# Zeroing the gate buffers beside the scans and the output projection, and more expert tiles beside each head's search, in a hybrid encoder block with product-key experts

## The chip, the core and the metric

One core of a Trainium2 chip runs the whole kernel. Its engines are TensorE (PE, matmul; PEld its weight loads), VectorE (DVE), ScalarE (ACT), GpSimd (POOL) and SyncE (SP). SP, ACT and GpSimd also issue DMAs, which 16 DMA engines carry out. The metric is the device time of one execution in microseconds.

## What is computed

One layer over 1024 tokens of width 1024, in float32. Four heads of a gated delta rule and four of an mLSTM are scanned forward and backward in chunks; then come an output projection and a layer of single-neuron experts that are found by product keys:

```
h = rmsnorm(x); p = h @ w_in                     # gq gk gv gz, mq mk mv mo and small gates
y = concat(gdn(conv(gq,gk,gv), gz), mlstm(mq,mk,mv,mo))   # chunked, both directions summed
x = x + y @ w_out
h2 = rmsnorm(x)
for each of 8 heads:                             # peer
    s = (h2 @ w_q) @ sub_keys                    # 2 x 128 scores a token
    16 best of each half -> 16 best of their sums: idx in 128*128, gate = softmax(best)
x = x + sum over heads and picks: gate * gelu(h2 . u_tab[idx]) * v_tab[idx]
out = rmsnorm(x)
```

## The kernel before

The 1024 tokens are eight blocks of 128. The kernel text is a plain sequence, but the builder reorders it: a planner with a model of each engine and queue sets the order in which each engine's instructions stand, and every engine then runs its own list in that order, waiting on semaphores. Two means in the text bind the planner: `tc.issue_after(x)` puts what is issued inside it behind instruction x on its engine's list, and `tc.keep_in_program_order` keeps a GpSimd DMA in the order of the text.

Front. `split_w` (L109) loads 128 columns of w_in, splits them into a high and a low part (`whi` on ACT at L116, `wlo` on GpSimd at L120), and 48 matmuls into two tiles `psP` make a projection (L127, three products for every pair). `conv_tile` (L401) evicts them to `xp`, and DVE runs the five-tap conv as five operations (L408, L412). For the delta rule's k and q, `to_rows` transposes (`psR`, L420), DVE normalises, and `psB` (L441) transposes back. `amat` (L449) then makes, for each chunk n, products `pkk` and `pqk`, and for each direction a unit: loads `dec` and `bb` from the row buffer rowb (three buffers each), GpSimd adds a mask (L460), ACT takes four exponentials (L463), GpSimd multiplies (L464), DVE multiplies with `pkk` and `pqk` (L465, L470), and ACT issues six stores (L466 to L471). `invert` (L481) inverts 32-wide diagonal blocks on DVE in 31 dependent steps, for the first four chunks and then for the last four, and stores them in `yinv`. Projections for mk, mq, the two output gates, mv and gv follow. Then `levels` (tiles `psX`, `psI`) completes the inverses, one step ahead of the scans `delta` (L625) and `mlstm` (L693), 8 steps in 2 directions. `project` (L823) makes the output projection and the second norm, block by block.

Expert stage. The blocks have two kinds. For two of them (AL) each token's 2 x 128 expert rows are gathered by GpSimd (`gather`, L1011) and summed on DVE. The other six (BL) use all 16384 experts densely: for each of 128 tiles i of 128 experts, `act_steps` (L1072) multiplies the split tile of u_t (`uh` on ACT, `ul` on DVE) with the blocks' transposed h2 in 48 matmuls `pa`, ACT takes the gelu, and the result is stored in gesc; `early_tile` is one such tile. Their gates form matrices of expert by token. For four of the six (NS = 4) these lie in DRAM as `gd`, which has to be zero at first; GpSimd scatters 8 x 16 x 4 = 512 columns into them (`scatter`, L1110). For the last two, `psg` matmuls build them.

`router_topk` does the search of a set of blocks, head by head: `scores` (matmuls `psq` with a split w_q, `pss` with the keys), then `between(h)`, then `select`, a long chain on DVE with two products `gm` on GpSimd (L956). `between` is where expert tiles and scatters are put beside a head: KTILE = 3 tiles a head for BL, each with KSCAT / KTILE = 7 scatters of the heads before; ATILE = 1 tile a head for AL, with ASCAT = 7 scatters. That makes 24 and 8 tiles. The 96 tiles left come after, each with USCAT = 3.3 scatters and UGATH = 1.8 gathers, the first 64 of them woven among the `psg` matmuls. The output phase then loads gesc and the gates tile by tile (`gt` from `gd`) and multiplies with v, the matmuls `held` and `po`.

The zeroing: `fills` lists 32 pieces of gd of 1 MB, and `fill(n)` (L102) issues n of them on ACT's queue from a zero tile. Each of the 32 weight splits called with the name w issues one, behind its `whi` copy.

Of the kernel before, what the change touches and what calls it, by code (L numbers as in the profile page):

```python
# [8 lines left out]
F32 = mybir.dt.float32  # L9
# [5 lines left out]
AF = mybir.ActivationFunctionType  # L15
# [3 lines left out]
P = 128  # L19
# [13 lines left out]
GPAD = 16  # L33
HELD = 3
VROWS = 4
ATILE, KTILE = 1, 3
KSCAT, ASCAT, USCAT = 21, 7, 3.3
UGATH = 1.8
OTOK = 4
PACE = 8  # L40
PSG, ATB, BTB = 4, 11, 6
# [21 lines left out]
def kernel(ctx, tc, x, norm1_g, w_in, conv_w, gdn_a_log, gdn_dt_bias, gdn_norm_g,  # L63
# [3 lines left out]
    V, A, G, T = nc.vector, nc.scalar, nc.gpsimd, nc.tensor  # L67
    dma = nc.sync.dma_start
    dmas = nc.scalar.dma_start
# [21 lines left out]
    cst = pool(ctx, "cst")  # L91
    ident = cst.tile([P, P], F32, name="ident")
    epsc = cst.tile([P, 1], F32, name="epsc")
    V.memset(epsc, EPS)
    tcol = cst.tile([P, 1], F32, name="tcol")
    G.iota(tcol, pattern=[[0, 1]], base=0, channel_multiplier=1, allow_small_or_imprecise_dtypes=True)
# [2 lines left out]
    gd = [scratch(f"gd{b}", [P * PITCH, 1]) for b in range(NS)]  # L99
    fills = [(b, i) for b in range(NS) for i in range(0, NK, 16)]  # L100

    def fill(n):  # L102

        for b, i in fills[:n]:
            dmas(gd[b].rearrange("(j c) o -> j (c o)", j=P)[:, i * P:(i + 16) * P].rearrange("j (a c) -> j a c", c=512),
                 zero[:, None, :].to_broadcast([P, 4, 512]))
        del fills[:n]

    def split_w(pl, src, c0, n, name="w", bufs=2, rbufs=2, raw=None):  # L109

        if raw is None:
            raw = pl.tile([P, KD, n], F32, name=f"{name}raw", bufs=rbufs)
        dma(raw, src[:, c0:c0 + n].rearrange("(k p) c -> p k c", p=P))
        hi = pl.tile([P, KD, n], F32R, name=f"{name}hi", bufs=bufs)
        lo = pl.tile([P, KD, n], F32R, name=f"{name}lo", bufs=bufs)
        cp = A.copy(hi, raw).ins  # L116
        if name == "w":
            with tc.issue_after(cp):
                fill(1)
        G.tensor_tensor(lo, raw, hi.bitcast(F32), op=OP.subtract)  # L120
        return hi, lo

# [32 lines left out]
    with ExitStack() as st:  # L155
# [6 lines left out]
        for l in (0, 5, 6, 7):  # L162
            a = tp.tile([P, P], I32, name=f"a{l}")
            b = tp.tile([P, P], I32, name=f"b{l}")
# [43 lines left out]
    with ExitStack() as st:  # L208
# [8 lines left out]
        for t in range(NT):  # L217
            xt = fr.tile([P, D], F32, name="xt", bufs=4)
# [4 lines left out]
            ssq = fr.tile([P, 1], F32, name="ssq", bufs=4)  # L223
# [26 lines left out]
        dma(gat, gsb)  # L250

    wp = pool(st_p, "wp", side="right")
    zero = wp.tile([P, 512], F32, name="zero")
    G.memset(zero, 0.0)
    st_w = ExitStack()
    wx = pool(st_w, "wx", side="right")
    gq = ExitStack()
# [367 lines left out]
    def delta(step, d):  # L625
        Y = Ys[step, d]
        n = chunk_of(d, step)
# [20 lines left out]
        for h in range(NH):  # L648
            T.matmul(pv[:, h], Y[:, h], R[:, h], start=True, stop=True)
        vn = gw.tile([P, NH, P], F32, name="vn")  # L650
        A.copy(vn, pv)
        yield
        if step < NT - 1:
            kd = gw.tile([P, NH, P], F32, name="kd")
# [131 lines left out]
    with ExitStack() as st:  # L786
# [36 lines left out]
        def project(t, yh, yl):  # L823
            xt = wo.tile([P, D], F32, name="xt", bufs=2)
            dma(xt, x2d[t * P:(t + 1) * P])
            for c in range(2):
                ps = pp.tile([P, 512], F32, name="psO", tag="pp")
                cl = slice(c * 512, c * 512 + 512)
                mm3(ps, lambda k: yh[:, k], lambda k: yl[:, k],
                    lambda k: woh[:, k, cl], lambda k: wol[:, k, cl], KD)  # L830
                V.tensor_tensor(xt[:, cl], ps, xt[:, cl], op=OP.add)
            dmas(x2sc[t * P:(t + 1) * P], xt)
            ssq = wo.tile([P, 1], F32, name="ssq", bufs=2)
            h2 = wo.tile([P, D], F32, name="h2", bufs=2)
            A.activation(h2, xt, AF.Square, accum_out=ssq)
            A.activation(ssq, ssq, AF.Sqrt, bias=epsc, scale=1.0 / D)
            V.reciprocal(ssq, ssq)
            V.scalar_tensor_tensor(h2, xt, ssq, g2b, op0=OP.mult, op1=OP.mult)
            dmas(h2sc[t * P:(t + 1) * P], h2)
            return h2  # L840
# [501 lines left out]
```

## Time and profile before

| | |
|---|---|
| median of 3 runs | 3634.5 us (3631.62 to 3637.68) |
| the profiled execution | 3634.53 us, span of its records 3632.8 us |
| mean granted TensorE clock | 0.941 |
| busy: PE, PEld, DVE, ACT, POOL | 89%, 79%, 63%, 26%, 54% of the span |
| DMA | 745.85 MB, 205 GB/s |

Times inside the profile count from the span's start. A row of the windows gives, for one stretch, how long each engine was busy, the clock that was granted to TensorE as a share of its full speed, and the mean share that 16 DMA engines were busy. A row of a group gives the count, the busy time and the mean of one, and behind the bar how long the engine stood idle just ahead of such instructions and what ended that; "issue" means that nothing the profile shows was waited for. Matmuls overlap, so the mean of one is longer than its step in a row of many; the step is the length of such a row over its count.

### The profile page before, as it was taken

To read this page: it belongs to the slowest core of one execution; us is meant where nothing else is said; L and a number is where in the kernel's file an instruction comes from. 1 tells how busy PE (TensorE), PEld (TensorE's weight loads), DVE (VectorE), ACT (ScalarE), POOL (GpSimd) and SP (SyncE) were. 2 spreads that over 40 slices of the span, in tenths; PEclk is the share of its full clock that TensorE was granted. 3 is DMA by queue.
4 is the path that set the end of the run, shared out by engine and by line. 5 is a ranking of instruction groups with operands and counts; after the bars stand their busy time and mean duration, and the time that the engine had idled before them with its cause. 6 is when DMAs were issued, how large, how long until landed. Compare 5 with 4: busy or idle time off the path is not lost.

```text
span 3632.8 us, 46554 instructions
## 1 busy us (share of the span) xinstructions
PE 3216.3 (89%) x16847; PEld 2887.7 (79%) x16847; DVE 2304.2 (63%) x4978; ACT 933.9 (26%) x1406; POOL 1974.0 (54%) x1379
## 2 busy tenths in 40 slices
PE   7752799998996788859999998998999999999998
PEld 5541678987896788759999998998788888888887
DVE  5343803467475797965555454334788888889886
ACT  4431123424232222322222222111212212222121
POOL 1202221444168885988787787887334444444552
PEclk9865899999998899879999999999999999999999
DMA  4425365665433443447877767777999999999994
GB/s 133 134 79 129 120 197 165 174 174 167 163 69 65 73 78 90 98 103 205 235 202 221 227 178 226 207 212 231 354 329 329 330 340 334 333 322 342 342 329 174
DMA packets 489303, 745.85 MB, mean 205 GB/s; under 512 B 126480, under 2 KB 315344, under 8 KB 488560
## 3 DMA queue, kind: packets, MB, share of 16 engines
q1 hardware_dynamic: 271984, 335.68, 29.1%
q0 software_dynamic: 147456, 268.76, 26.4%
q10 hardware_dynamic: 69632, 138.43, 10.3%
q8 instruction: 132, 2.16, 0.3%
q14 instruction: 99, 0.81, 0.1%
HBM read 603.82 MB, written 138.90 MB: 204 GB/s over the span
## 4 chain that ended last, share of the span: by engine, by line
PE 56%; POOL 13%; DMA 12%; DVE 11%; issue 6%; ACT 2%; ACTq 0%; SPq 0%; DVEq 0%; POOLq 0%
PE po L1270 15%; PE held L1270 15%; PE pa L1078 10%; POOL gd L1112 10%; PE psP L127 7%; DMA g<-in_peer_u_dram,idxA 5%; PE psO L127 2%; PE psq L127 2%; POOL g L1013 2%; DVE pq L497 1%; DMA dec<-rowb 1%; POOL gm L956 1%; DMA g<-in_peer_v_dram,idxA 1%; DMA gd<-gateB,idxB 1%; DVE ul L1069 1%
## 5 line engine op out<-in xcount | busy, mean ns | idle before, releaser
L1112 POOL DMA_INDIRECT gd<-gateB,idxB x512 | 887.4, 1733 | 183.4 <-issue 143.9
L1078 PE MATMUL pa<-h2Th,ul 128*128 128x384 f32 x2048 | 537.3, 343 | 85.8 <-DVE ul L1069 85.8
L1013 POOL DMA_INDIRECT g<-in_peer_v_dram,idxA x256 | 372.9, 1457 | 413.9 <-DVE ac L1038 363.6
L1078 PE MATMUL pa<-h2Th,uh 128*128 128x384 f32 x2048 | 558.1, 354 | 0.5 <-ACT uh L1068 0.5
L1078 PE MATMUL pa<-h2Tl,uh 128*128 128x384 f32 x2048 | 533.2, 341 | 0.0
L1022 DVE CUSTOM_DVE_ANT_0 g<-g,h2A 128x1024 f32<-128x1024 f32 x256 | 311.8, 1223 | 312.2 <-DMA g<-in_peer_u_dram,idxA 312.1
L1078 PEld LDWEIGHTS pa<-h2Th,ul 128*128 128x128 f32 x2048 | 377.1, 192 | 94.1 <-DVE ul L1069 94.1
L1013 POOL DMA_INDIRECT g<-in_peer_u_dram,idxA x256 | 312.1, 1219 | 218.7 <-DVE act L1022 161.5
L1078 PEld LDWEIGHTS pa<-h2Tl,uh 128*128 128x128 f32 x2048 | 379.1, 192 | 0.0
L1038 DVE SCALAR_TENSOR_TENSOR ac<-g,act,ac 128x1024 f32<-128x1024 f32 x254 | 325.6, 1282 | 76.5 <-DMA g<-in_peer_v_dram,idxA 74.9
L1078 PEld LDWEIGHTS pa<-h2Th,uh 128*128 128x128 f32 x2048 | 363.0, 193 | 1.2 <-ACT uh L1068 1.2
L1240 ACT CAST wh<-g 128x768 fp32r<-128x768 f32 x128 | 106.4, 832 | 779.0 <-PE po L1270 629.8
L120 POOL TENSOR_TENSOR wlo<-wraw,whi 128x1024 fp32r<-128x1024 f32 x32 | 80.0, 2501 | 334.0 <-ACT whi L116 306.2
L1068 ACT CAST uh<-g 128x1024 fp32r<-128x1024 f32 x128 | 134.3, 1049 | 434.8 <-PE pa L1078 399.5
L127 PE MATMUL psP<-hTh,whi 128*128 128x512 f32 x512 | 207.2, 405 | 39.6 <-ACT mkT L521 32.4
L1270 PE MATMUL po<-h2Tl,wh 128*128 128x512 f32 x576 | 227.3, 395 | 0.0
L1270 PE MATMUL po<-h2Th,wl 128*128 128x512 f32 x576 | 227.3, 395 | 0.0
L1270 PE MATMUL po<-h2Th,wh 128*128 128x512 f32 x576 | 227.2, 394 | 0.0
L1270 PE MATMUL held<-h2Tl,wh 128*128 128x512 f32 x576 | 226.3, 394 | 0.0
L1270 PE MATMUL held<-h2Th,wl 128*128 128x512 f32 x576 | 225.8, 395 | 0.0
L1270 PE MATMUL held<-h2Th,wh 128*128 128x512 f32 x576 | 222.8, 394 | 0.0
L127 PE MATMUL psP<-hTh,wlo 128*128 128x512 f32 x512 | 205.1, 401 | 9.5 <-POOL wlo L120 9.5
(387 smaller groups left out, 6558.8 us busy)
## 6 DMA issues: line engine op xcount, KB each, us to landing
g<-in_u_t_dram SPq DMA_DIRECT2D x128, 512.0 KB, 4.2
g<-in_peer_v_dram SPq DMA_DIRECT2D x128, 512.0 KB, 6.9
gesc<-ge ACTq DMA_DIRECT2D x128, 384.0 KB, 5.3
g<-gesc SPq DMA_DIRECT2D x128, 384.0 KB, 6.2
gd<-zero ACTq DMA_DIRECT2D x32, 1024.0 KB, 4.3
gt<-gd SPq DMA_DIRECT2D x256, 128.0 KB, 6.6
wraw<-in_w_in_dram SPq DMA_DIRECT2D x32, 512.0 KB, 5.2
g<-in_peer_wq_dram SPq DMA_DIRECT2D x32, 512.0 KB, 4.3
```

The costliest lines, as they stand in the source:

```text
L120: G.tensor_tensor(lo, raw, hi.bitcast(F32), op=OP.subtract)
L127: T.matmul(ps, a(i), b(i), start=(k == 0), stop=(k == 3 * nk - 1))
L497: V.tensor_tensor(prod, U[:, row:row + 1, sp].to_broadcast([P, i, i]), Y[:, sp, sp].rearrange("p c k -> p k c"), op=OP.mult)
L956: G.tensor_tensor(m.rearrange("p r (b k) -> p r b k", k=TOPK), ge.rearrange("p r (b k) -> p r b k", k=TOPK), dix[:, :, which].rearrange("p ...
L1013: tc.keep_in_program_order(G.indirect_dma_start(out=g, out_offset=None, in_=tab, in_offset=bass.IndirectOffsetOnAxis(ap=idxA[:, b, k // TO ...
L1022: V.tensor_tensor_reduce(out=g, in0=g, in1=h2A, op0=OP.mult, op1=OP.add, scale=1.0, scalar=0.0, accum_out=acts[b][:, k:k + 1])
L1038: V.scalar_tensor_tensor(accs[b], g, w, accs[b], op0=OP.mult, op1=OP.add)
L1068: last_act.append(A.copy(uh, ur).ins)
L1078: T.matmul(pa[:, half, :HB], a[:, k], b[:, k, half * HB:half * HB + HB], start=(k == 0 and m == 0), stop=(k == KD - 1 and m == 2))
L1112: tc.keep_in_program_order(G.indirect_dma_start(out=gd[b], out_offset=bass.IndirectOffsetOnAxis(ap=idxB[:, b, h, k:k + 1], axis=0), in_=ga ...
L1240: last_act.append(A.copy(wh, ge).ins)
L1270: T.matmul(po, a[:, tl], b[:, cl], start=(m == 0 and (q == 0 or not mine)), stop=(m == last and (q == NG - 1 or not mine)))
```

## The change

The fills leave `split_w`. Each of the 16 `delta` calls issues one behind its copy `vn`, and each of the 8 `project` calls issues two behind its Square. The zero tile is half as wide and stands in the pool of constants, so that a fill is written in pieces of 1 KB and not of 2 KB. Four expert tiles instead of three go beside each head of the six-block search, with 24 scatters a head instead of 21; two instead of one beside each head of the two-block search, with 2 x 5 = 10 scatters instead of 7. So 48 tiles are done by then instead of 32, and 80 are left, each with 3.3 scatters as before and 2.1 gathers.

```
-ATILE, KTILE = 1, 3
-KSCAT, ASCAT, USCAT = 21, 7, 3.3
-UGATH = 1.8
+ATILE, KTILE = 2, 4
+KSCAT, ASCAT, USCAT = 24, 5, 3.3
+UGATH = 2.1
...
     epsc = cst.tile([P, 1], F32, name="epsc")
+    zero = cst.tile([P, 256], F32, name="zero")
+    G.memset(zero, 0.0)
...
-    def fill(n):
+    def fill(n, ins):
         for b, i in fills[:n]:
-            dmas(gd[b].rearrange("(j c) o -> j (c o)", j=P)[:, i * P:(i + 16) * P].rearrange("j (a c) -> j a c", c=512),
-                 zero[:, None, :].to_broadcast([P, 4, 512]))
+          with tc.issue_after(ins):
+            dmas(gd[b].rearrange("(j c) o -> j (c o)", j=P)[:, i * P:(i + 16) * P].rearrange("j (a c) -> j a c", c=256),
+                 zero[:, None, :].to_broadcast([P, 8, 256]))
         del fills[:n]
...
-        cp = A.copy(hi, raw).ins
-        if name == "w":
-            with tc.issue_after(cp):
-                fill(1)
+        A.copy(hi, raw)
...
     wp = pool(st_p, "wp", side="right")
-    zero = wp.tile([P, 512], F32, name="zero")
-    G.memset(zero, 0.0)
...
         vn = gw.tile([P, NH, P], F32, name="vn")
-        A.copy(vn, pv)
+        fill(1, A.copy(vn, pv).ins)
...
-            A.activation(h2, xt, AF.Square, accum_out=ssq)
+            fill(2, A.activation(h2, xt, AF.Square, accum_out=ssq).ins)
```

The planner's order moves with it, most of all where no line was edited. Its lines stand two lower in numbers there (L463 is L461). The first place is ACT's list in the decay stage. `dec` are the exponentials of a unit, atsc, dinv and qksc its stores, mqT and cv evictions of projections, whi a weight's split. Before:

```order
L463 ACTIVATE dec<-dec,gcol 128x128 x8
L466 DMA atsc<-bb 128x512
L469 DMA dinv<-bb 32x4x32 x4
L471 DMA qksc<-dec 128x512
L466 DMA atsc<-bb 128x512
L469 DMA dinv<-bb 32x4x32 x4
L471 DMA qksc<-dec 128x512
```

And now:

```order
L461 ACT_TABLE_LOAD
L461 ACTIVATE dec<-dec,gcol 128x128 x4
L519 ACTIVATE mqT<-psP 128x512
L533 ACT_TABLE_LOAD
L533 ACTIVATE cv<-psP 128x512
L119 CAST whi<-wraw 128x1024
L461 ACT_TABLE_LOAD
L461 ACTIVATE dec<-dec,gcol 128x128 x4
L464 DMA atsc<-bb 128x512
L467 DMA dinv<-bb 32x4x32 x4
L469 DMA qksc<-dec 128x512
```

Projections and weight splits that stood behind all units now stand among them; between the first and the last qksc there are 15 table loads where there was 1, and 7 splits where there was none.

The second place is GpSimd's list in a later head of the six-block search, where gd is a scatter, gm a product of `select` and wqlo a weight's split. Before:

```order
L120 TENSOR_TENSOR wqlo<-g,wqhi 128x1024 x2
L1112 DMA gd<-gateB,idxB 2228224x1 x19
L956 TENSOR_TENSOR gm<-ge,dix 128x1536
L1112 DMA gd<-gateB,idxB 2228224x1 x2
L956 TENSOR_TENSOR gm<-ge,dix 128x1536
```

And now:

```order
L120 TENSOR_TENSOR wqlo<-g,wqhi 128x1024 x2
L1110 DMA gd<-gateB,idxB 2228224x1 x19
L954 TENSOR_TENSOR gm<-ge,dix 128x1536
L1110 DMA gd<-gateB,idxB 2228224x1 x4
L954 TENSOR_TENSOR gm<-ge,dix 128x1536
L1110 DMA gd<-gateB,idxB 2228224x1
```

Each head has three scatters more, two of them ahead of its second gm. In the two-block search a head's list is now two wqlo, ten scatters and two gm side by side.

The third place is DVE's list where one head's `select` ends and the next one's begins (jsel, selB and idxB end it, the maxima v begin it). Before:

```order
L960 TENSOR_REDUCE jsel<-gm 128x96
L1142 COPY selB<-jsel 128x2x16
L1144 SCALAR_TENSOR_TENSOR idxB<-jsel,isel 128x4x16
L893 MAX v<-sc 128x8 x6
L894 MAX_INDEX ix<-v,sc 128x8
```

And now:

```order
L958 TENSOR_REDUCE jsel<-gm 128x96
L1140 COPY selB<-jsel 128x2x16
L1142 SCALAR_TENSOR_TENSOR idxB<-jsel,isel 128x4x16
L1067 TENSOR_TENSOR ul<-g,uh 128x1024
L891 MAX v<-sc 128x8 x6
L892 MAX_INDEX ix<-v,sc 128x8
```

The `ul` of the added tile stands between two heads; before, none stood there and the next came 38 rows later.

## Rows read from the trace of the kernel before

**Rows 1.** Windows: stretch in us and its length, busy us (and instructions) of PE, PEld, DVE, ACT and POOL, granted TensorE clock, share of the DMA engines, GB/s.

```profile
107.00:254.00 147.00, 101.04 (x449) 81.87 (x449) 63.39 (x87) 62.85 (x98) 27.54 (x14) 0.79 0.37 107
254.00:387.00 133.00, 25.65 (x128) 24.24 (x127) 54.74 (x92) 18.83 (x55) 32.95 (x26) 0.54 0.50 127
387.00:652.00 265.00, 261.42 (x1200) 215.87 (x1200) 90.97 (x100) 72.93 (x102) 57.93 (x35) 0.99 0.52 165
652.00:860.00 208.00, 188.10 (x1610) 183.71 (x1609) 131.34 (x394) 77.46 (x202) 92.55 (x88) 0.96 0.60 168
860.00:965.00 105.00, 100.88 (x481) 83.42 (x480) 61.59 (x100) 38.53 (x79) 29.21 (x60) 0.98 0.48 161
...
1033.00:1378.00 345.00, 284.15 (x1605) 281.90 (x1603) 244.76 (x1044) 81.62 (x114) 302.65 (x171) 0.92 0.40 69
...
1425.00:1578.00 153.00, 129.47 (x795) 125.39 (x795) 131.69 (x534) 58.81 (x85) 138.63 (x92) 0.89 0.48 111
1578.00:2236.00 658.00, 607.69 (x3593) 603.82 (x3594) 352.95 (x870) 153.61 (x202) 529.07 (x335) 0.96 0.71 201
2236.00:2517.00 281.00, 257.57 (x1424) 251.82 (x1423) 100.26 (x122) 51.81 (x60) 229.69 (x151) 0.98 0.74 210
```

**Rows 2.** Waits of TensorE from 107 to 387 us: who waited for whom, total us, times, longest.

```profile
PE pkk L453 <- DVE bb L465: 75.3, 5, 19.2
PE psB L441 <- DVE rows L436: 32.5, 8, 6.1
PE psP L127 <- POOL wlo L120: 6.2, 1, 6.2
PE psP L127 <- ACT xp L406: 4.4, 1, 4.4
PE psP L127 <- ACT whi L116: 2.9, 1, 2.9
```

**Rows 3.** The chain of work in the decay stage: start, us, what.

```profile
267.23 9.60 DMA dec<-rowb
```

**Rows 4.** The same chain just ahead of the scans: 45 projection matmuls in a row, the last ones.

```profile
641.83 10.39 PE psP L127 x45
```

**Rows 5.** Groups of TensorE from 107 to 254 us.

```profile
L441 PE MATMUL psB<-ident,rows 128*128 128x128 f32 x64 | 13.1, 342 | 32.5 <-DVE rows L436 32.5
L420 PE MATMUL psR<-ident,cv 128*128 128x128 f32 x64 | 12.9, 338 | 0.0
```

**Rows 6.** Single lines over the whole span: count, duration in ns (least, median, most), start of the first and of the last, in us; and the landing of yinv.

```profile
L453 PE MATMUL pkk<-kT x64: 274/421/554, 253.7 to 352.8; 128*128 128x128 f32 x64
...
L465 DVE TENSOR_TENSOR bb<-pkk,bb x16: 669/688/692, 255.8 to 381.4; 128x512 f32<-128x512 f32 x16
...
L463 ACT ACT_TABLE_LOAD  x2: 1283/1283/1283, 119.5 to 267.7; - x2
...
L501 ACTq DMA_DIRECT2D yinv<-Yd x2: 452/478/503, 394.0 to 451.8; - x2
...
DMA to landing us min/median/max: 3.1/3.1/3.1
...
L412 DVE SCALAR_TENSOR_TENSOR cv<-xp,cw,cv x48: 1269/1284/2830, 67.2 to 605.4; 128x1022 f32<-128x1022 f32 x24, 128x1023 f32<-128x1023 f32 x24
...
L574 PE MATMUL psX<-ident,Y x16: 270/273/273, 611.9 to 630.2; 128*128 128x128 f32 x16
...
L587 PE MATMUL psX<-Y,Pm x32: 217/275/276, 623.8 to 641.6; 128*128 128x64 f32 x32
```

**Rows 7.** DMA queues over the span (q1 is SP's, q10 ACT's): packets, MB, share of 16 engines; then the issue of the fills on ACT and their time to landing.

```profile
q1 hardware_dynamic: 271984, 335.68, 29.1%
...
q10 hardware_dynamic: 69632, 138.43, 10.3%
...
L105 ACTq DMA_DIRECT2D gd<-zero x32: 366/366/475, 20.0 to 623.8; - x32
...
DMA to landing us min/median/max: 4.2/4.3/12.7
```

**Rows 8.** Groups of GpSimd from 1033 to 1378 us.

```profile
L1112 POOL DMA_INDIRECT gd<-gateB,idxB x147 | 240.5, 1636 | 45.9 <-issue 41.4 <-DMA kyT<-in_peer_keys_dram 3.6 <-PE psq L127 0.6
```

**Rows 9.** Group and wait of GpSimd from 1378 to 1578 us.

```profile
L1112 POOL DMA_INDIRECT gd<-gateB,idxB x53 | 88.7, 1673 | 13.4 <-issue 11.9 <-DVE ul L1069 0.3 <-DVE tk L896 0.3
...
POOL gm L956 <- DVE ge L954: 34.2, 2, 26.0
```

**Rows 10.** Groups of GpSimd from 1578 to 2517 us.

```profile
L1112 POOL DMA_INDIRECT gd<-gateB,idxB x312 | 558.3, 1789 | 124.1 <-issue 90.5 <-DMA gd<-gateB,idxB 32.3 <-DMA g<-in_peer_u_dram,idxA 1.2
L1013 POOL DMA_INDIRECT g<-in_peer_u_dram,idxA x152 | 177.7, 1169 | 51.4 <-issue 29.9 <-DVE bt L1195 7.3 <-DVE at L1194 5.8
L1013 POOL DMA_INDIRECT g<-in_peer_v_dram,idxA x16 | 18.1, 1133 | 4.9 <-issue 4.3 <-DVE ul L1069 0.6
```

**Rows 11.** Group of TensorE from 1033 to 1378 us.

```profile
L1078 PE MATMUL pa<-h2Th,ul 128*128 128x384 f32 x288 | 79.5, 359 | 60.9 <-DVE ul L1069 60.9
```

**Rows 12.** Waits for loads in the scans (650 to 860 us).

```profile
POOL Wt L699 <- DMA Wt<-rowb: 20.6, 6, 6.8
...
POOL kd L656 <- DMA kd<-ksc: 8.3, 6, 2.4
```

**Rows 13.** Single lines over the span, as rows 6: the scatters, and the gelu that ends each expert tile.

```profile
L1112 POOL DMA_INDIRECT gd<-gateB,idxB x512: 1546/1574/3898, 1032.7 to 2514.6; - x171
...
L1083 ACT ACTIVATE ge<-pa x128: 792/805/821, 1002.3 to 2536.0; 128x768 f32<-128x768 f32 x128
```

**Rows 14.** DMA issues of the page: engine, count, KB each where known, median us from issue to landing.

```profile
gd<-gateB,idxB POOLq DMA_INDIRECT x512, 4.0
...
gt<-gd SPq DMA_DIRECT2D x256, 128.0 KB, 6.6
```

## The prediction

> **What bounds the kernel now.** I read the table of windows first, to cut the span into stages with one limit each; then, stage by stage, the waits of the engine that should be full, and the groups of instructions by line for the price of one. The stage cuts are those of the windows [rows 1]: projections and conv (107 to 254), decay matrices (254 to 387), the other projections (387 to 652), scans (652 to 860), output projection (860 to 965), the search of the six gate-matrix blocks with its expert tiles (1033 to 1378), the search of the two gathered blocks (1425 to 1578), the building of gates with the remaining expert tiles (1578 to 2517), the output phase from about 2540 on.
>
> Two stages are not bound by TensorE. From 254 to 387 it is busy for 25.7 of 133 us at a granted clock of 0.54 [rows 1]; it waits 75.3 us for DVE's products bb, and 32.5 us before that for conv rows [rows 2]. What limits there is a ring of three buffers whose load from rowb alone takes 9.60 us [rows 3]. Then, from 387 to 652, TensorE is busy for 261.4 of 265 us: the projections that could have filled the hole come after it.
>
> The second is the stretch from 1033 to 2517, and its limit is GpSimd. In 1033 to 1378 its 302.7 us of busy time [rows 1] and the 45.9 us in front of its scatters, nearly all "issue" [rows 8], are more than the 345 us there are: it never waits for another engine. In 1578 to 2517, 558.3 + 124.1 us for scatters and some 250 for gathers [rows 10] fill the 939 us. TensorE's idle time in the heads is a wait for `ul` (60.9 us, [rows 11]), an instruction in DVE's order behind sums that wait for GpSimd's `gm`. GpSimd holds up the rest.
>
> **The change, part by part.** The profiled execution took 3634.53 us, the median is 3634.5; the sum is made against that.
>
> *The order of the projections.* The fills leave the weight splits, and with them the planner's order changes: the order now has 811 projection matmuls ahead of the first `pkk` instead of 528 and 224 more between the first `pkk` and the last `pqk` (none before); 549 are left behind instead of 1056. TensorE's work is the same; the hole is what can go. I follow the chain that ends the stage:
> - From 107 us, where 205 of them are done, 606 at 0.231 (10.39/45, [rows 4]) are 140 us; 128 transposes at 0.203 ((13.1 + 12.9)/128, [rows 5]) 26; the waits for POOL and ACT stay, 13.5 [rows 2]; the 32.5 us for rows are covered by projections now. First `pkk` at 286 instead of 253.7 [rows 6].
> - The 16 units run from 255.8 to 381.4 [rows 6], 125.6 us. Now 14 more ACT table loads at 1.283 [rows 6] stand between their exponentials: +18. The last product bb is at 286 + 2 + 126 + 18 = 432.
> - From the last bb to the second inversion's result it is 451.8 - 381.4 = 70 us [rows 6]. 20 conv operations now stand inside it on DVE, at up to 1.284 [rows 6]: +26. That is 528, landed (3.1, [rows 6]) 531.
> - The first scan step's levels took from 611.9 to 641.6 [rows 6], 30 us; 23 projection matmuls come after them, 5 us. The scans begin at 566 instead of 652.2 [rows 4]: **-86**.
>
> TensorE alone would be done earlier: last `pqk` at 286 + 99 + 18 = 403, 549 matmuls 127, 64 transposes 13, so 543: **-109** is the upper end. The lower end is all 224 matmuls of the ring's stretch (52 us) ahead of its exponentials and not beside them, 52 - 18 = 34 more: **-52**. I take the chain, which follows the in-order engines row by row.
>
> *The fills, now in the scans and the output projection.* ACT's queue moved 138.43 MB for 10.3% of sixteen engines' span [rows 7]: 2.70 us a megabyte. 16 fills are 43 us of the engines' time, in scans of 208 us with a share of 0.60 (83 us free), and 43 again in an output projection of 105 us with 0.48 (55 free) [rows 1]. Both fit, and TensorE is busy for 188 of 208 and 101 of 105 us there. In the scans GpSimd waits for loads of Wt and kd 28.9 us in all [rows 12]; if these grow by the added load, 43/(0.60 x 208) = 0.34, it is 10, and some four tenths of that reaches TensorE: +4. +3 for the output projection, where two last fills run beside the first loads of the search. The bounds are 0 and 32 x 2.70 = 86; I take +7, near the lower, since the free share covers them. Where the fills stood before, 387 to 652 is TensorE's own time, so nothing comes back but what the order gives. A fill's issue costs ACT 0.366 us either way [rows 7], and ACT is busy for 77 of 208 us in the scans [rows 1]. The smaller `zero`, its memset moved to the start: nothing, it precedes all use.
>
> The pieces of a fill shrink from 2 KB to 1 KB. The row nearest to that is SP's queue, mostly of small pieces: 335.68 MB for 29.1% [rows 7], 3.15 us a megabyte. By that price 32 fills cost 14 us more of the engines' time than by ACT's, still inside the free share, so the 7 stands. The Trainium skill (Perfetto Trace Analysis, DMA Optimizations) speaks against the change here: it says that transfers under 2 KB carry a significant overhead each. The two queues' rows agree in direction, at 17% a megabyte.
>
> *Tiles and scatters beside the heads.* Eight tiles more go beside the six-block search, eight beside the two-block one, sixteen fewer come after. If GpSimd limits, tiles cost nothing and only its instructions count. Six-block search: 168 scatters instead of 147, 21 at 1.95 ((240.5 + 45.9)/147, [rows 8]): +41. Two-block search: 80 instead of 56, 24 at 1.93 ((88.7 + 13.4)/53, [rows 9]): +46, and 8 more because the order now puts both `gm` of a head side by side, a microsecond's wait for DVE each time. The rest: 45 fewer at 2.19 (682.4/312, [rows 10]), -99, and two gathers fewer ahead of the last scatter at 1.5, -3. Together -8 at GpSimd's end. The fourth `ul` at the head's start costs DVE nothing that counts: it works 244.8 of 345 us [rows 1].
>
> *The hand-over.* Before, the last scatter starts at 2514.6, TensorE's last tile leaves ACT from 2536.0 on [rows 13]: scatters ran out early (3.3 x 96 is over 309). Now 3.3 x 80 is just 264, so the last one goes with the last tile, and the gates wait for it: landing 4.0, the load of gt 6.6 [rows 14], some 4 for product and split, 15 us after GpSimd's end instead of 21. -6; together with the above **-14**.
>
> The far ends: the 32.3 us that the scatters' group waits for DMA [rows 10] vanish, -46; or each of eight heads waits for DVE between its two `gm` as long as the shorter of the two waits of before (34.2 in two, the longer 26.0: 8.2, [rows 9]), +58 net of the 8.
>
> **The sum:** -86 + 7 - 14 = -93: **3541.5 us**.
>
> **Rivals.**
> - *TensorE limits the search* (chance 0.10). It idles 61 of 345 and 24 of 153 us there [rows 1]; if 16 tiles at 10.0 us each ((2536 - 1578)/96) fill that hole, they cost 160 - 85 = 75 and the rest shrinks by 160: -85 in place of -8, **3464 us**. For it: the new `ul` stands right where TensorE waited. Against it: GpSimd's row without a wait.
> - *The new order gives nothing back* (0.07). The ring and the inversion stretch by what the projections save, since ACT and DVE now do both in one order: 3541.5 + 86 = **3627 us**. For it: three engines in one order each; against it: ACT is busy for 18.8 of 133 us there [rows 1].
> - *Pieces of 1 KB cost double* (0.07). A fill takes 5.4 us of all engines: 86 against 83 free in the scans, 86 against 55 free in the output projection: +34, **3575 us**. This is where the rule above would lead.
> - *Each fill holds up its stage* (0.04), the side of slower. The fills share the engines with the loads that the scans wait for; if the chain waits out each fill's landing, and not a tenth of it, the price per fill decides: above (93 + 7)/32 = 3.1 us the change loses. At the 12.7 us of the slowest landing and 4.2 of the quickest [rows 7] the kernel is slower either way; at 4.2, 3534.5 + 134 = **3669 us**. Against it: both stages have free share, and most loads are two buffers ahead.
> - That the fills come too late for the scatters is no case: the last is issued near 960, the first scatter starts at 1032.7 [rows 13].
>
> **How the numbers follow.** My forecast has 0.72. The change can be told from none beyond 0.2%, 7 us. Faster: the forecast, TensorE and 1 KB cases and a third of the order case, 0.91; same 0.05; slower 0.04. The range takes in the order's ends (-52 to -109) with GpSimd's nearer half (-46 to +20) and the fills up to +20: 3470 to 3590; TensorE's case, the slower one and the order's rest lie outside.
>
> **What would show it.** Right: the first `pkk` near 286 and TensorE busy for over half of the decay stage; the scans' first matmul near 566, their length as before; heads of the six-block search GpSimd-bound with no wait but "issue", some 6 us longer each; the stretch from the first `psg` to the output phase some 100 us shorter. Wrong: scans or output projection longer by over 20 us with waits for DMA; a scan start after 620; or the search no longer than before, which would say that TensorE was the limit.

## The result, and the profile after

The changed kernel took **3524.2 us** (median of 4 runs, 3523.7 to 3529.7) against 3633.1 (4 runs, 3627.4 to 3637.7) of the kernel before, beside which it ran: a ratio of 0.9705, 95% interval 0.9687 to 0.9722. The forecast was 3541.5 within 3470 to 3590. The profiled execution took 3524.66 us, its span is 3522.9, 109.9 less than the span before.

The windows of the kernel after, the stages cut where the same events fall; columns as in [rows 1]:

```profile
262.00:396.00 134.00, 99.17 (x467) 82.50 (x466) 54.83 (x89) 54.97 (x94) 49.33 (x33) 0.87 0.75 164
396.00:530.00 134.00, 122.68 (x578) 101.35 (x577) 86.14 (x103) 40.01 (x56) 32.07 (x24) 0.95 0.39 111
530.00:749.00 219.00, 193.84 (x1619) 188.22 (x1617) 134.91 (x397) 78.35 (x204) 93.32 (x89) 0.94 0.76 234
749.00:867.00 118.00, 103.16 (x483) 85.04 (x481) 60.86 (x100) 40.92 (x81) 26.85 (x60) 0.93 0.85 292
932.00:1368.00 436.00, 386.39 (x2170) 382.82 (x2169) 283.37 (x1230) 105.93 (x144) 352.97 (x201) 0.94 0.39 75
1368.00:1603.00 235.00, 198.72 (x1215) 195.62 (x1214) 147.77 (x606) 80.77 (x114) 208.83 (x167) 0.93 0.50 117
...
2260.00:2417.00 157.00, 142.01 (x778) 139.42 (x776) 57.60 (x66) 27.32 (x32) 126.87 (x84) 0.97 0.74 212
```

In the decay stage (262 to 396) TensorE is busy for 99 of 134 us where it was for 26 of 133, at a clock of 0.87 and not 0.54. Scans and output projection last 219 and 118 us at DMA shares of 0.76 and 0.85. TensorE's waits from 90 to 396 us, to be set beside [rows 2], and single lines beside [rows 6]:

```profile
PE pkk L451 <- DVE bb L463: 18.6, 4, 8.2
PE psB L439 <- DVE rows L434: 14.6, 1, 14.6
PE psR L418 <- DVE bb L463: 13.9, 1, 13.9
```

```profile
L451 PE MATMUL pkk<-kT x64: 271/275/553, 261.5 to 353.5; 128*128 128x128 f32 x64
L463 DVE TENSOR_TENSOR bb<-pkk,bb x16: 681/691/692, 262.7 to 395.1; 128x512 f32<-128x512 f32 x16
L572 PE MATMUL psX<-ident,Y x16: 270/272/278, 493.3 to 513.9; 128*128 128x128 f32 x16
```

The wait of pkk for bb is a quarter of what it was (with the one of psR, under half), and the levels `psX` begin at 493 and not 612. GpSimd's scatters in the six-block search, the two-block search and the rest (932 to 1368, 1368 to 1603, 1603 to 2417), beside [rows 8 to 10], and TensorE's wait of [rows 11]:

```profile
L1110 POOL DMA_INDIRECT gd<-gateB,idxB x168 | 280.9, 1672 | 52.9 <-issue 47.4 <-DVE idxB L1142 3.6 <-DMA gd<-gateB,idxB 1.8
```

```profile
L1110 POOL DMA_INDIRECT gd<-gateB,idxB x87 | 146.5, 1684 | 24.8 <-issue 22.9 <-PE psq L127 0.6 <-PE pss L918 0.3
```

```profile
L1110 POOL DMA_INDIRECT gd<-gateB,idxB x257 | 458.3, 1783 | 100.3 <-issue 74.1 <-DMA gd<-gateB,idxB 25.6 <-DMA g<-in_peer_u_dram,idxA 0.6
```

```profile
L1076 PE MATMUL pa<-h2Th,ul 128*128 128x384 f32 x452 | 123.3, 355 | 49.6 <-DVE ul L1067 49.5
```

A scatter still costs 1.7 to 1.8 us and some 0.3 of issue, and TensorE still waits for ul. The table has the stages of every kernel run here, from its profiled execution, in us. "Front" is the first psR to the end of the last psP; "scans" is the first psI to the first psO, "output projection" from there to the first psq; "six" is the first scatter to the sixteenth product gm with dix (two a head, eight heads), "two" from there to the thirty-second, "rest" from there to the end of the last scatter, "sum" these three.

| kernel | first psR | front | scans | output projection | six | two | rest | sum | span |
|---|---|---|---|---|---|---|---|---|---|
| before | 107.2 | 545.0 | 210.2 | 106.1 | 387.8 | 188.6 | 908.0 | 1484.4 | 3632.8 |
| after | 90.3 | 440.1 | 218.7 | 117.9 | 435.5 | 235.2 | 813.7 | 1484.3 | 3522.9 |
| e1 zero small | 99.7 | 433.0 | 211.9 | 106.2 | 387.8 | 189.8 | 907.2 | 1484.7 | 3520.0 |
| e2 room 1 KB | 89.1 | 543.7 | 219.4 | 118.8 | 436.7 | 234.2 | 811.3 | 1482.2 | 3625.5 |
| e3 fills only | 89.1 | 435.2 | 218.1 | 118.2 | 389.3 | 188.7 | 904.7 | 1482.8 | 3521.8 |
| e4 tiles only | 100.7 | 541.6 | 209.4 | 107.0 | 436.3 | 234.4 | 815.1 | 1485.8 | 3621.0 |
| e5 late fills | 88.6 | 431.3 | 210.0 | 107.1 | 433.4 | 233.9 | 809.4 | 1476.8 | 3490.8 |
| e6 fills behind | 88.6 | 439.4 | 222.2 | 112.1 | 435.8 | 234.8 | 816.9 | 1487.6 | 3522.7 |
| e7 tiles, no scatters | 89.7 | 437.4 | 215.8 | 117.8 | 402.4 | 202.2 | 891.5 | 1496.2 | 3540.3 |
| e8 scatters, no tiles | 88.4 | 436.7 | 220.3 | 118.8 | 425.5 | 194.5 | 865.1 | 1485.2 | 3524.4 |
| e9 wqlo on DVE | 88.1 | 432.1 | 209.7 | 107.1 | 404.7 | 221.3 | 808.6 | 1434.6 | 3442.7 |
| e10 gm on DVE | 87.8 | 432.0 | 208.9 | 106.6 | 369.9 | 189.1 | 817.9 | 1376.8 | 3390.1 |
| e11 pieces of 512 B | 88.4 | 436.2 | 220.0 | 127.5 | 436.2 | 235.0 | 810.2 | 1481.4 | 3520.6 |
| e12 more scatters | 88.1 | 431.8 | 208.3 | 106.7 | 369.3 | 188.9 | 783.0 | 1341.2 | 3350.3 |

From before to after the last psP ends 121.8 us earlier (652.2 to 530.4). Scans and output projection give back 8.5 and 11.8. The GpSimd stretch moves 47.7 and 46.6 us into the searches and 94.3 out of the rest, and its sum stays. The hand-over to the output phase stays, and that phase is 9 us shorter (1093.7 to 1084.8).

### The profile page after: what moved, and what is told of

It reads as the page before. It is cut to its first block, busy times and chain, and to the rows that moved or that the text cites. A ratio compares the mean times of both kernels' runs of the same rounds, so it can differ in the third digit from the quotient of the medians.

```text
span 3522.9 us, 46531 instructions
## 1 busy us (share of the span) xinstructions
PE 3217.6 (91%) x16847; PEld 2893.4 (82%) x16847; DVE 2278.9 (65%) x4978; ACT 953.2 (27%) x1420; POOL 2000.4 (57%) x1379
## 3 DMA queue, kind: packets, MB, share of 16 engines
q10 hardware_dynamic: 86016, 138.43, 10.8%
## 4 chain that ended last, share of the span: by engine, by line
PE 51%; DMA 16%; POOL 13%; DVE 11%; issue 7%; ACT 1%; ACTq 0%; SPq 0%; DVEq 0%; POOLq 0%
PE po L1268 15%; PE held L1268 15%; POOL gd L1110 9%; PE pa L1076 7%; DMA g<-in_peer_u_dram,idxA 5%; PE psP L127 5%; DMA gd<-gateB,idxB 3%; PE psq L127 3%; POOL g L1011 2%; DVE ul L1067 1%; PE psO L127 1%; POOL gm L954 1%; DVE pq L495 1%; POOL wqlo L120 1%; DVE cv L410 1%
## 5 line engine op out<-in xcount | busy, mean ns | idle before, releaser
L1011 POOL DMA_INDIRECT g<-in_peer_v_dram,idxA x256 | 388.0, 1516 | 376.0 <-DVE ac L1036 330.2
L1076 PE MATMUL pa<-h2Th,uh 128*128 128x384 f32 x2048 | 566.0, 358 | 1.9 <-ACT uh L1066 1.9
L1011 POOL DMA_INDIRECT g<-in_peer_u_dram,idxA x256 | 324.1, 1266 | 244.6 <-DVE act L1020 188.5
L1076 PEld LDWEIGHTS pa<-h2Th,uh 128*128 128x128 f32 x2048 | 369.3, 196 | 2.4 <-ACT uh L1066 2.4
L127 PE MATMUL psP<-hTl,whi 128*128 128x512 f32 x512 | 205.8, 402 | 0.0
```

What stands on the lines that cost most here:

```text
L127: T.matmul(ps, a(i), b(i), start=(k == 0), stop=(k == 3 * nk - 1))
L1011: tc.keep_in_program_order(G.indirect_dma_start(out=g, out_offset=None, in_=tab, in_offset=bass.IndirectOffsetOnAxis(ap=idxA[:, b, k // TO ...
L1076: T.matmul(pa[:, half, :HB], a[:, k], b[:, k, half * HB:half * HB + HB], start=(k == 0 and m == 0), stop=(k == KD - 1 and m == 2))
```

## The experiments

**What opened the order (e1, e2).** The diff does two things to the front: the fills leave the splits, and a tile of 2 KB a partition leaves the pool `wp`, for one of 1 KB in the constants. A view that the prediction did not draw on, ACT's waits in the kernel before (355 to 480 us), points at one of them:

```profile
ACT mqT L521 <- DVE pq L500: 18.6, 1, 18.6
...
ACT mkT L521 <- DMA qksc<-dec: 8.7, 1, 8.7
...
ACT mqT L521 <- DMA Y<-yinv: 8.2, 1, 8.2
ACT mkT L521 <- DVE pq L500: 6.5, 1, 6.5
```

The evictions of the mk and mq projections wait for pq, for the store of dec and for Y, none of which they read. The likely reason is memory: the pool of mkT and mqT (L521) is opened in the text where those of the decay and inversion stages are closed, so its tiles can stand where theirs stood, and then no order can put those projections earlier. With 1 KB more they need not share. (The traces hold no addresses; e1 and e2 put it to the test.) After the change no eviction of mkT or mqT has such a wait in the whole span, only those for psP; from 230 to 560 us there is one group of them:

```profile
ACT mqT L519 <- PE psP L127: 7.5, 3, 4.1
```

e1, on the kernel before (fills at the splits, tiles 3 and 1):

```diff
-    zero = wp.tile([P, 512], F32, name="zero")
+    zero = wp.tile([P, 256], F32, name="zero")
...                  # and in fill: c=256, to_broadcast([P, 8, 256])
```

> The kernel before with one edit: the zero tile is 1 KB a partition instead of 2 KB, where it stood, and a fill is written in pieces of 1 KB. The fills stay at the weight splits, the tiles beside the heads stay 3 and 1. Theory A (memory): the freed 1 KB a partition lets the evictions mkT and mqT stop sharing memory with tiles of the decay stage, so the projections move in among the units; the planner's order has 811 projection matmuls ahead of the first pkk instead of 528. The last psP then ends about 105 us earlier (the 122 of the change, less the 17 by which its first psR came earlier), scans and output projection keep their 210 and 106 us, the expert stage its length: about 3634 - 105 = 3529 us, 3515 to 3540. Theory B (the fills' leaving the splits opened the order, as the prediction had it): nothing moves, 3634 us, or a little above if the 1 KB pieces cost something.

Measured: 3521.8 us, ratio to before 0.9718 (0.9697 to 0.9739), as Theory A had it. The halved zero tile, with no fill and no expert tile moved, gives as much as the whole change.

e2, on the changed kernel:

```diff
     wp = pool(st_p, "wp", side="right")
+    room = wp.tile([P, 256], F32, name="room")
+    G.memset(room, 0.0)
```

> The changed kernel with one edit: an unused tile of 1 KB a partition stands where the zero tile stood, so that the memory of the front is as full as before, while the fills are at the scans and the output projection and the tiles beside the heads are 4 and 2. Theory A (memory): the projections are kept behind the units again (528 matmuls ahead of the first pkk); what is left of the change is the earlier first psR (-17), the fills' price (+9 in the scans, +12 in the output projection) and the moved tiles (-8 with the output phase's start): about 3634 - 4 = 3630 us, 3615 to 3640. Theory B (the fills' leaving the splits opened the order): as the changed kernel, 3524 us.

Measured: 3629.1 us, ratio 1.0013 (0.9998 to 1.0028). This is Theory A again: all else of the change, without the freed kilobyte, gives nothing that can be measured in the whole (an earlier first psR, and longer scans and output projection, nearly cancel). The traces count the order: 528 matmuls psP start ahead of the first pkk before the change and in e2, 811 after it and in e1. In e2 two of the old waits are back (ACT, 230 to 560 us):

```profile
ACT mqT L521 <- DVE pq L500: 17.6, 1, 17.6
...
ACT mkT L521 <- DMA qksc<-dec: 8.7, 1, 8.7
```

and so is the hole in TensorE's work, here the decay stage of e2 and then of e1 (windows, columns as before):

```profile
236.80:362.30 125.50, 25.05 (x129) 23.64 (x128) 50.31 (x88) 18.47 (x54) 33.14 (x26) 0.55 0.56 130
```

```profile
270.00:410.00 140.00, 110.86 (x508) 91.26 (x507) 59.25 (x90) 57.17 (x98) 52.01 (x33) 0.89 0.75 213
```

**The two halves apart (e3, e4).** e3 is the changed kernel with the numbers of tiles put back, e4 the kernel before with the new ones:

```diff
-ATILE, KTILE = 2, 4                  # e3, from after; e4 is the reverse, from before
-KSCAT, ASCAT, USCAT = 24, 5, 3.3
-UGATH = 2.1
+ATILE, KTILE = 1, 3
+KSCAT, ASCAT, USCAT = 21, 7, 3.3
+UGATH = 1.8
```

> The changed kernel with the tiles and scatters put back to 3 and 1 tiles, 21 and 7 scatters a head. Theory A (GpSimd's scatters set the pace of the whole search and of what follows): the moved tiles are worth next to nothing, the sum over the stretches of the changed kernel being about +2 to -8 us, so 3524 to 3533 us, with the six-block search back at 385 us, the two-block search at 189, the rest at 910. Theory C (TensorE limits the search, and 16 tiles less behind it are a gain of 77): 3601 us.

Measured: 3526.3 us, ratio 0.9728 (0.9705 to 0.975).

> The kernel before with the tiles and scatters of the change alone (4 and 2 tiles, 24 and 5 scatters, 2.1 gathers), zero tile and fills as before. Theory A (GpSimd's scatters set the pace): the six-block search about 47 us longer, the two-block search 49 longer, the rest 95 shorter, the sum about +2; with up to 9 us less at the start of the output phase 3625 to 3637 us. Theory C (TensorE limits the search): 77 us less, 3557 us.

Measured: 3624.3 us, ratio 0.9995 (0.9982 to 1.0007). Theory A fits both: the moved tiles and scatters are worth nothing, with the order open or not: 436 + 234 + 815 in place of 388 + 189 + 908.

**What a fill costs, and where (e5, e6, e11).** e5 takes the fills out of scans and output projection and lets the splits issue them again, but late:

```diff
+        cp = A.copy(hi, raw).ins
+        if name == "w":
+            splits += 1
+            fill(0 if splits <= 6 else 2 if splits <= 12 else 1, cp)
...                  # splits counts the calls; the fills behind vn and Square go
```

> The changed kernel with the fills put back to the weight splits, but none at the first six splits, two at each of the next six and one at each of the last 20, so that they start some 130 us into the span, after the first psR, and are done before the scans. The order of the projections stays open. Theory A (a fill costs where its stage leaves the DMA queues little room, and the projections between 130 and 530 us leave enough): first psR stays at 90, the scans go back from 219 to 211 us and the output projection from 118 to 106, so 3524 - 20 = 3504 us, 3497 to 3512. Theory B (the 32 MB cost about 20 us wherever they are put): 3524 us, with the 20 us now in the projections.

Measured: 3501.1 us, ratio 0.966 (0.9636 to 0.9683), against 0.9705 of the change: Theory A. Scans and output projection are back at 210.0 and 107.1 us, first psR stays at 88.6, the front is not longer. (Its profiled execution, 3492.6 us, is the shortest of its four, the one of e6, 3524.5, the longest of its four; so their spans are not to be compared.) e5 also shows what the change got at its start: with a fill at each of the first splits (e1, e4) the first psR stands at 99.7 and 100.7, with none there at 88 to 90.

In the output projection the fills stand on ACT's queue between a block's two stores, and h2 has two buffers. The chain of work of the kernel after shows it (start, us, what), and ACT's wait:

```profile
779.00 7.83 DMA yg<-ygate
786.83 15.44 DMA h2sc<-h
```

```profile
ACT h L833 <- DMA h2sc<-h: 9.1, 1, 9.1
```

e6 puts them behind the second store:

```diff
-            fill(2, A.activation(h2, xt, AF.Square, accum_out=ssq).ins)
+            A.activation(h2, xt, AF.Square, accum_out=ssq)
...
-            dmas(h2sc[t * P:(t + 1) * P], h2)
+            fill(2, dmas(h2sc[t * P:(t + 1) * P], h2).ins)
```

> The changed kernel with one edit: in the output projection a block's two fills are issued behind its store of h2 and not ahead of it; the scans' fills stay. Theory A (what the fills cost there is h2's store, which stands behind 2 MB on ACT's queue while two buffers of h2 are all there are): the waits for h2sc go, the output projection falls from 118 to some 109 us, 3515 us. Theory B (the cost is the shared DMA engines, 0.85 busy, whatever stands first on the queue): the output projection stays at 118 us, 3524 us.

Measured: 3510.6 us (3506.0 to 3524.5), ratio 0.9675 (0.9654 to 0.9695), which cannot be told from the change's. The stage says more: 112.1 us, half of the 11.8 gone. Two waits show why not all: the next blocks' stores still stand behind fills, and ACT itself stands idle by "issue" while it issues fills and the stores behind them (one store's issue takes 4.9 us there).

```profile
ACT yh L817 <- issue: 14.1, 1, 14.1
...
ACT h L833 <- DMA h2sc<-h: 7.9, 1, 7.9
```

So the order on ACT's queue is part of the price. How much of the other half is the queue and how much the loaded engines stays open. e11 doubles the pieces of the changed kernel:

```diff
-    zero = cst.tile([P, 256], F32, name="zero")
+    zero = cst.tile([P, 128], F32, name="zero")
...                  # and in fill: c=128, to_broadcast([P, 16, 128])
```

> The changed kernel with one edit: the zero tile is 512 B a partition and a fill is written in pieces of 512 B, twice as many as in the changed kernel; every engine's list is the same. Theory A (a fill costs by its bytes): scans 219 and output projection 118 us as in the changed kernel, 3524 us, 3518 to 3530. Theory B (a piece costs by its number): the packets of the ACT queue take markedly more time, and the fills' 9 and 12 us become some 17 and 24: 3545 us.

Measured: 3524.3 us, ratio 0.9718 (0.9693 to 0.9744), no change in the whole; but the output projection takes 127.5 us and not the 117.8 to 118.8 of the five kernels with fills of 1 KB pieces there ahead of the store, while the scans stay at 220. That is between the theories. ACT's issues show the place: the 32 fills of the kernel after and those of e11 (ns of an issue: least, median, most). In the output projection ACT's idle time by "issue" adds up to 17 us in the kernel after, 39 in e11 and none in e5, which has no fill there.

```profile
L108 ACTq DMA_DIRECT2D gd<-zero x32: 366/409/4447, 541.1 to 858.6; - x32
```

```profile
L108 ACTq DMA_DIRECT2D gd<-zero x32: 366/1116/6728, 535.3 to 859.3; - x32
```

**What the moved tiles and scatters do (e7, e8).** Since both together are worth nothing, they were moved apart. e7 moves the tiles alone, e8 the scatters alone:

```diff
-KSCAT, ASCAT, USCAT = 24, 5, 3.3     # e7, on after (4 and 2 tiles)
+KSCAT, ASCAT, USCAT = 21, 3.5, 4.0
...
-KSCAT, ASCAT, USCAT = 21, 7, 3.3     # e8, on e3 (3 and 1 tiles)
+KSCAT, ASCAT, USCAT = 24, 10, 2.75
```

> The changed kernel with its 4 and 2 expert tiles beside the heads, but 21 and 7 scatters a head as before the change (4.0 scatters for each later tile). Theory A (GpSimd's scatters set the pace of the search, TensorE has the room for the tiles): six-block search about 395 us and not 435, two-block search about 200 and not 235, the rest about 825 and not 814, since TensorE has the same 755 us to do there and GpSimd about 730; 3524 - 65 = 3459 us, 3445 to 3490. Theory C (the added tiles' matmuls are what lengthened the search): 435 and 235 us stay, 3524 us. Theory D (the scatters that are left over limit the rest): the rest goes to 880 or more, 3510 us or more.

Measured: 3547.3 us, ratio 0.9784 (0.9765 to 0.9804): 23 us slower than the change. The searches came as Theory A had them (402 and 202 us), so most of the added matmuls fit beside GpSimd. Not all do: with the same scatters and fewer tiles (e3) each search is 13 us shorter, and TensorE is busy for 379 of the 402 us. The rest came as Theory D had it, 891.5 and not 825, though TensorE's busy time in it is only 762. The rest, too, goes by the scatters: 301 in it here, 257 in the changed kernel, 77.8 us for 44, 1.8 each.

> The changed kernel with 3 and 1 expert tiles beside the heads as before the change, but its 24 and 10 scatters a head (2.75 scatters and 1.8 gathers for each later tile). Theory A (GpSimd's scatters set the pace of the search): six-block search about 432 us, two-block search about 235, the rest about 890, where TensorE has 865 us to do; 3524 + 75 = 3600 us, 3580 to 3610. Theory C (the added tiles' matmuls are what lengthened the search): 389, 189 and 890 to 905 us, 3510 to 3526 us.

Measured: 3529.7 us, ratio 0.9735 (0.9715 to 0.9755), and neither theory: the six-block search grew to 425.5 us as forecast, but the two-block search ended after 71 scatters and not 87, at 194.5, and the rest, of 273 scatters, took 865.1, where TensorE is nearly full:

```profile
1549.60:2414.70 865.10, 854.40 (x5052) 853.45 (x5053) 445.73 (x934) 204.41 (x254) 686.32 (x445) 0.99 0.76 222
```

GpSimd is as full there: its scatters and gathers and the idle time ahead of them add up to 865 us too, so this run does not part the two engines in the rest. With one tile a head the two-block search takes 188.7 us for 64 scatters (e3) and 194.5 for 71 (e8), with two tiles 202.2 for 64 (e7) and 235.2 for 87 (after): it goes by both, by scatters the more. GpSimd's work is the same in the ten kernels up to here and in e11, and the sum of the three stretches stays between 1477 and 1496 us in all of them. If GpSimd's work sets that sum, moving tiles and scatters has to leave it where it was.

**Taking work off GpSimd (e9, e10, e12).** If that holds, the sum falls when GpSimd has less to do. e9 and e10 give two of its instructions to DVE, on top of e5:

```diff
-        G.tensor_tensor(lo, raw, hi.bitcast(F32), op=OP.subtract)                          # e9
+        (V if name == "wq" else G).tensor_tensor(lo, raw, hi.bitcast(F32), op=OP.subtract)
...
-                G.tensor_tensor(m.rearrange("p r (b k) -> p r b k", k=TOPK),               # e10
+                V.tensor_tensor(m.rearrange("p r (b k) -> p r b k", k=TOPK),
```

> e5_late_fills with one edit: the low parts of the w_q splits (wqlo, 32 times 2.95 us on GpSimd in the changed kernel) are made on DVE, where an instruction of the same shape (wol in the output projection) took 1.84 us. Theory A (from the first scatter to the last GpSimd has a fixed stock of work, and that stock sets the sum of the three stretches): about 83 us of wqlo inside the stretches go, TensorE still fits (386 + 199 + 754 us busy of 1484), 3501 - 65 = 3436 us, 3420 to 3460. Theory E (the selection chain on DVE sets the length of a head): DVE gets 59 us more and the stretches grow by about 40 to 50: 3545 us.

Measured: 3448.7 us, ratio 0.951 (0.9484 to 0.9536). The sum fell by 42 us where GpSimd's busy time in it fell by 67 (1215 in e5, 1148 here): Theory A, though less than forecast. Why the other 25 us do not come out stays open. DVE's greater load lengthened no stage.

> e9_wqlo_dve with one edit more: the two products gm of the selection are made on DVE too (in the changed kernel 16 of 3.5 us and 16 of 1.4 to 1.6 us on GpSimd, and DVE waited some 216 us for them in the two searches, since scatters stood ahead of them; products of the same shapes on DVE, gm<-ge,dof_c, took 1.35 and 0.42 us). Theory A (GpSimd's stock): another 80 us of work and 34 us of waits for ge leave GpSimd, so that TensorE's 1340 us become the floor of the three stretches: 3501 - 125 = 3376 us, 3355 to 3420. Theory E (DVE's chain): with 28 us more on DVE and no hand-over to GpSimd inside a head, heads are shorter by the waits and not by the stock; the searches then fall, the rest stays at 810 us or grows by the scatters that the searches no longer take.

Measured: 3391.5 us, ratio 0.9348 (0.9322 to 0.9373). The sum fell by another 58 us, more than the 41 that left GpSimd. That is within Theory A's range, but the searches fell and the rest grew by 9 us, as Theory E had it; so less work and no hand-over are not told apart here. In the changed kernel DVE waits for gm, which stands behind scatters on GpSimd (932 to 1603 us):

```profile
DVE isel L958 <- POOL gm L954: 167.8, 14, 31.8
DVE jsel L958 <- POOL gm L954: 48.5, 8, 7.0
```

Without that hand-over TensorE is busy in every microsecond of both searches of e10, so it limits them now. In the rest it is not; whether GpSimd sets that is put to the test in e12. The three stretches of e10:

```profile
900.30:1270.10 369.80, 369.80 (x2161) 369.80 (x2160) 298.84 (x1255) 104.56 (x143) 315.43 (x228) 1.00 0.47 89
1270.10:1459.20 189.10, 189.10 (x1225) 189.03 (x1224) 152.12 (x638) 79.03 (x107) 129.24 (x79) 1.00 0.59 140
1459.20:2277.10 817.90, 755.72 (x4363) 748.72 (x4362) 416.89 (x911) 179.96 (x231) 662.52 (x422) 0.96 0.74 214
```

GpSimd has room now in the two-block search (129 of 189 us), and e12 fills it, on e10:

```diff
-KSCAT, ASCAT, USCAT = 24, 5, 3.3
+KSCAT, ASCAT, USCAT = 24, 6, 3.1
```

> e10_gm_dve with one edit: 6 scatters and not 5 with each tile of the two-block search (12 a head and not 10), and 3.1 and not 3.3 with each later tile. In e10_gm_dve TensorE is busy for all 189 us of the two-block search while GpSimd stands idle in 36 us of it, and in the 818 us of the rest TensorE is busy for 756 and GpSimd's 258 scatters set the end. Theory A (GpSimd's stock is what counts, and only its idle time can be filled): 16 scatters go from the rest into that idle time, at about 2 us each; two-block search about 192 us, the rest about 786, 3391 - 29 = 3362 us, 3350 to 3380. Theory E (DVE's or TensorE's chain sets the rest): 818 us stay, 3391 us.

Measured: **3356.7 us**, ratio 0.925 (0.9235 to 0.9266), the fastest kernel here, and Theory A. The two-block search did not grow, and the rest, with 241 scatters and not 257, fell by 35 us: GpSimd's scatters set it, and not the chain of DVE or of TensorE.

```profile
1269.50:1458.40 188.90, 188.90 (x1225) 188.83 (x1224) 152.11 (x637) 79.03 (x107) 159.52 (x96) 1.00 0.62 140
1458.40:2241.40 783.00, 746.23 (x4360) 742.46 (x4359) 418.18 (x912) 179.93 (x231) 636.00 (x406) 0.97 0.76 224
```

## Why the prediction was right, and where it was wrong

**The two limits** it named were the right ones. TensorE stood idle in the decay stage [rows 1, 2] and stopped doing so. GpSimd's scatters set the searches [rows 8, 9]: the forecast lengthened the six-block search by 41 us and the two-block search by 54 and shortened the rest by 102; measured 47.7, 46.6 and 94.3, a sum of -0.1 and not -8 (the forecast's own terms add up to -7). e7 and e12 add that the rest goes by scatters too.

**The cause of the order is the step that failed:** "The fills leave the weight splits, and with them the planner's order changes". With the fills at the splits the order opens (e1), with the fills away and the kilobyte taken it does not (e2). The orders of the two kernels showed what moved and not why; the waits of evictions on tiles they never read, in the trace of before, pointed to it. The time came out because the built order was known, whatever had caused it.

**Its size** was -86 and is -121.8 at the last psP, outside the bounds of -52 to -109 (without the earlier first psR it is -105, inside them). Its terms were off to both sides. The first psR came 17 us earlier in this pair of profiles (11 between e1 and e5, which differ in the fills at the splits); the sum had that at zero, having looked for room for the fills only from 387 us on and not ahead of 107. And the ring of units kept most of its pace, from the first bb to the last 132 us and not 144 (126 before): with 14 table loads among them the units took 7 us more and not 18. The first pkk came 171 us after the first psR (179 forecast), yinv 87 after the last bb (96). Against that, from yinv to the last psP it took 48 us where the sum had 38.

**The fills** were sized +7 and cost 20.3: +8.5 in the scans (+4 forecast) and +11.8 in the output projection (+3). "The free share covers them" failed in the second: a mean share of 0.85 from 749 to 867 us does not keep a store from waiting behind two fills on its own queue, nor ACT from being held at their issue. In the scans the waits named did not grow: those of GpSimd for Wt and kd were 28.9 us [rows 12] and are 20.4. Its waits for R (of vsc) grew from 3.5 to 26.1 us, but e5, whose scans took 210, has 29.2 of them. Where the 8.5 us come from stays open. Per fill the 20.3 us are 0.6, far from the 3.1 at which the change would lose.

**The hand-over** was to give 6 us and gave 0.4. Its content changed, not its length: before, the last expert tile filled it (TensorE busy for 19.9 us between 2517 and 2540), now TensorE waits 21.3 us for the first tile of v, from whose split on ACT it starts. The output phase, at nothing, gave 9. With the fills alone it took 1090.6 us (e3), with the tiles alone 1091.7 (e4), 1093.7 before; what shortens it stays open.

**So part of the nearness is luck.** The whole came out at -109.9 in the spans for a forecast of -93, because the terms' errors offset each other: the order gained 36 us more than forecast and the output phase 9, while the fills cost 13 more, and the tiles and the hand-over gained 8 and 6 less.

**The rivals.** TensorE as the limit of the searches: e3 and e4 show that the moved tiles bring no 85 us, e7 that TensorE had room for most of them. "The new order gives nothing back" did not happen, nor did each fill hold up its stage. For the pieces of 1 KB, ACT's queue tells: its 138.43 MB take 10.3% of 16 engines' span before [rows 7], and in the kernels after and e11:

```profile
q10 hardware_dynamic: 86016, 138.43, 10.8%
```

```profile
q10 hardware_dynamic: 118784, 138.43, 11.3%
```

From after to e11, with the same instruction lists, 32768 more pieces add 0.5% of 16 engines and some 3521 us, about 9 ns a piece, too little to double a fill's price. The Trainium skill (Perfetto Trace Analysis, DMA Optimizations) says that transfers under 2 KB carry a significant overhead each. The queue's rows here agree in direction, and the whole kernel's time does not show it. In e11 the output projection is some 10 us longer, and ACT is held at the issue for longer there.

## What to carry to other kernels

Where a change moves work that no line of it names, look first for waits of an instruction on something it does not read: two tiles may share memory there, and here 1 KB a partition was worth over 100 us. Where one engine's work sets several stages in a row, moving that work between them keeps the sum; take it off that engine, then fill the idle time that is left. Bulk stores are best put where no small store has to follow them on the same queue: e5 gave back the 20 us or so that the fills had cost.

## What the runs showed of the hardware

- Clock: where TensorE was busy throughout, in both searches of e10, the granted clock was 1.00, its level of 2.4 GHz; with gaps before ul and psq in the same stages of the kernel after it was 0.94 and 0.93. Its busy time in the two fell from 585 us (386.4 + 198.7) to 559 with it.
- An engine that issues DMAs can be held at the issue: a fill's issue on ACT took 366 ns at the median before [rows 7], at most 4447 ns in the scans and the output projection after, and 1116 at the median with pieces of 512 B (at most 6728); in e5, between 126 and 494 us, at most 645.
- By the traces a packet on ACT's queue took 88 ns in the mean with 2 KB (before), 48 with 1 KB (after) and 28 with 512 B (e11).
- The subtraction wqlo of 128 x 1024 took GpSimd 2.95 us at the median (after) and DVE 1.22 (e9); the product gm<-ge,dix of 128 x 1536 in bf16 took GpSimd 3.52 (after) and DVE 1.76 (e10).
